# One weight split listed earlier in VectorE's fixed order at the start of the down projection

## The chip, the cores and the metric

The kernel runs on one core of one Trainium2 chip. The metric is the device time of one execution in microseconds (us): a median of 1360.73 us over three runs, from 1359.66 to 1361.09. An execution was also profiled; its rows are quoted below. Line numbers such as L129 are lines of the kernel before; behind the change, the lines from 899 on stand three lower.

## The reference, cut to what matters

One layer of a hybrid encoder block: a short convolution beside an attention head group, an output projection, a gated MLP with a width-3 convolution over positions, a gated embedding, and a last norm. 1024 positions, 1024 channels, 2816 hidden channels of the MLP, all in float32.

```python
    x = x + jnp.concatenate([y_conv, y_mla], axis=-1) @ w_o[i]
    hf = rmsnorm(x, norm_ffn_g[i])
    a = dwconv_centred(hf @ w_up[i], ffn_conv_w[i], ffn_conv_b[i])
    g, u = jnp.split(a, 2, axis=-1)
    x = x + (jax.nn.silu(g) * u) @ w_down[i]
    gate = jax.nn.sigmoid(rmsnorm(x, ple_norm_g[i]) @ w_ple_gate[i])
    x = x + gate * (p[i] @ w_ple_proj[i])
    return rmsnorm(x, final_norm_g)
```

The change is in the line with `w_down`, the down projection, at its very beginning.

## The kernel before, in words

Activations lie transposed: channels on the 128 partitions, 1024 positions along the free axis. A float32 product is made of three products of a shorter type: each operand is split into a high part (a cast, done by ScalarE, ACT) and a low part (the value minus its high part, done by VectorE, DVE), and `gemm` issues high x high, high x low and low x high. With two halves of 512 positions, that is six matmuls per 128x128 block of weights, in this order: weight high with input high (twice), weight high with input low (twice), weight low with input high (twice).

The up projection computes 22 hidden chunks of 128 channels, one unit after the other. Each unit is seven products of sub-blocks (the steps 1 to 7 of a Strassen-like scheme) that go to PSUM banks; DVE adds the banks up (L790), the convolution takes one ACT and two DVE instructions (L261, L262, L263), DVE multiplies the two branches (L810), and SP (the sync engine's DMA queue) writes the chunk to a buffer `gud` in DRAM (L811). The last unit's step 4 comes last on TensorE (PE).

The down projection reads the chunks back in groups of 3, 3, 3, 3, 3, 3 and 4. For a group, `chunk(g)` loads one chunk into a tile `tmp` (L884) and splits it into two tiles `gu` (cast on ACT, L267; subtraction on DVE, L268). `pair(j)` loads the group's weights for two of the eight output tiles into a tile `wraw` (L120, three buffers) and splits them into `whi` (ACT, L128) and `wlo` (DVE, L129), two buffers each. For the first two output tiles the kernel first runs the group's chunks 0 and 1 for both, then chunk 2 for both; the other output tiles run all three chunks one after the other. The finished banks are added by DVE to the residual tiles `x0` to `x7` (L921), which the GpSimd queue (POOL) has loaded back from DRAM (L893).

What sets the order: PE runs in program order through the whole kernel. DVE is in program order too from L892 to the end of the first group (`order0`); each of its instructions keeps the place in which the code lists it, relative to others of that stretch. The compiler's list scheduler decides, by its own time model, how this list is merged with what is still open of the up projection, and it orders ACT, POOL and SP. [...]

The lines around the change: L896 to L898 make the group's chunks, L901 to L906 define `pair`, and L906 and L908 call `pair(0)` and, in the first group, `pair(1)`.

Of the kernel before, what the change touches and what calls it, by code (L numbers as in the profile page):

```python
# [33 lines left out]
def tile_block(ctx, tc, xT, pT, wlat, wun, wdn, wuq, wukv, vecs, cst, out):  # L34
# [25 lines left out]
    def ft(dt=F32, shape=None):  # L60
        return tpool[0].tile(shape or [P, S], dt, name="tmp")
# [12 lines left out]
    def pieces(acc):  # L74
        if isinstance(acc, list):
            return [(acc[i], HALF[i]) for i in range(2)]
        return [(acc, slice(0, S))]
# [37 lines left out]
    def vc(i):  # L115
        return vec[:, i:i + 1]
# [8 lines left out]
    def load_unit(src, n=1024, to=None):  # L125
        raw = load_raw(src, n)
        wh, wl = to or (wp.tile([P, n], FR, name="whi"), wp.tile([P, n], FR, name="wlo"))
        act(out=wh, in_=raw, func=AF.Copy)  # L128
        loeng[0].tensor_tensor(out=wl, in0=raw, in1=f(wh), op=ALU.subtract)  # L129
        return wh, wl  # L130
# [14 lines left out]
    def blocks(acc, w, base, xh, xl, ks, n):  # L145
        for k in ks:
            c = slice((base + k) * P, (base + k) * P + P)
            gemm(acc, w[0][:, c], w[1][:, c], xh[k], xl[k], k == 0, k == n - 1)
# [117 lines left out]
    def split(src, hi, lo, eng=None):  # L266
        nc.scalar.copy(out=hi, in_=src)  # L267
        (eng or nc.gpsimd).tensor_tensor(out=lo, in0=src, in1=f(hi), op=ALU.subtract)  # L268

    def split_gain(x, g, hi, lo):  # L270
        act(out=hi, in_=x, func=AF.Copy, scale=g)
        stt(out=lo, in0=x, scalar=g, in1=f(hi), op0=ALU.mult, op1=ALU.subtract)
# [36 lines left out]
    for c in range(NC_):  # L309
        raw = load_raw(wlat[c], 448)  # L310
        x = ft()
# [473 lines left out]
    def up_unit(c, later=None):  # L785
        raws = [load_raw(wun[U_UP + 2 * c + j]) for j in range(2)]
        mid = lambda n: sp.tile([P, n * 512], FR, name=f"wm{n}", bufs=6 if n == 2 else 4)
        a = stationary(raws[0], raws[1], 512, mid, lambda m: sp.tile([P, S], F32, name=m), later)
        ag, au = tmp.tile([P, S], F32, name="tmp"), tmp.tile([P, S], F32, name="tmp")
        add = lambda o, p, q: tt(out=o, in0=p, in1=q, op=ALU.add)  # L790
        out_, half = [], []

        def read(i, p):
            g1, g2, u1, u2 = ag[:, T1S], ag[:, T2S], au[:, T1S], au[:, T2S]
            if i == 1:
                nc.scalar.copy(out=u1, in_=p)
            elif i == 5:
                add(u2, p, u1)
            elif i == 2:
                nc.scalar.copy(out=g1, in_=p)  # L800
            elif i == 7:
                add(u2, p, u2)
            elif i in (3, 6):
                add(g2, p, g2 if half else u1)
                half.append(i)
            else:
                add(u1, p, u1)
                tpool[0] = tmpb
                t = conv3(au, V_FW + 6 * c + 3, V_FB + 2 * c + 1)
                tt(out=t, in0=out_[0], in1=t, op=ALU.mult)  # L810
                nc.sync.dma_start(out=gud[c], in_=t)  # L811
            if i in (3, 6) and len(half) == 2:
                tpool[0] = tmpb
                t = conv3(ag, V_FW + 6 * c, V_FB + 2 * c)
                act(out=t, in_=t, func=AF.Silu)
                out_.append(t)
        return Unit(a, hf, read)

    pair = [up_unit(0)]
# [14 lines left out]
    def bank():  # L834
        return pb.tile([P, 512], F32, name="bk")
# [39 lines left out]
    def gate_unit():  # L875
        d = len(wg)
        wg.append(load_unit(wun[U_GATE + d], to=(gt(), gt()) if d < 6 else None))
# [4 lines left out]
    def chunk(g):  # L882
        y = ft()
        nc.sync.dma_start(out=y, in_=gud[starts[g] + len(chunks[g])])  # L884
        chunks[g].append((gt(), gt()))
        split(y, *chunks[g][-1], nc.vector)
# [7 lines left out]
    for g, n in enumerate(GROUPS):  # L894
        last = g == len(GROUPS) - 1
        gu = chunks[g]  # L896
        while len(gu) < n:
            chunk(g)  # L898
        gh, gl = [x[0] for x in gu], [x[1] for x in gu]
        ws = []  # L900

        def pair(j):
            if j < 4:
                c = 2 * P * (4 * starts[g] + j * n)
                ws.append(load_unit(wdn[:, c:c + 2 * n * P], 2 * n * P))
        pair(0)  # L906
        if g == 0:
            pair(1)  # L908
        for d in range(NC_):
            if d % 2 == 0:  # L910
                if g and d:
                    pair(d // 2)
                w = ws[d // 2]
            if d == 0:
                p01 = [[bank(), bank()] for _ in range(2)]
                for i in range(2):
                    blocks(p01[i], w, i * n, gh, gl, range(2), n)
            p = p01[d] if d < 2 else [bank(), bank()]
            blocks(p, w, d % 2 * n, gh, gl, range(2 if d < 2 else 0, n), n)
            for q, s in pieces(p):  # L920
                tt(out=x1[d][:, s], in0=q, in1=x1[d][:, s], op=ALU.add)  # L921
            if g == 0 and d % 2:
                pair(d // 2 + 2)
            elif g == 0 and d:
                chunk(1)
            if last:
                hh.append(xp.tile([P, S], FR, name=f"hh{d}"))
                hl.append(xp.tile([P, S], FR, name=f"hl{d}"))
                split_gain(x1[d], vc(V_PLE + d), hh[d], hl[d])
                if d in (1, 3, 5):  # L930
                    gate_unit()
        if g == 0:
            order0.close()
# [214 lines left out]
```

## Time and profile before

| what | value |
|---|---|
| median of three runs | 1360.73 us (1359.66 to 1361.09) |
| the profiled execution, its own time | 1358.89 us |
| its span, first to last instruction | 1357.1 us |
| PE busy | 1322.0 us, 97% of the span |
| DVE busy | 1005.8 us, 74% |
| ACT busy | 597.2 us, 44% |
| POOL busy | 261.1 us, 19% |
| mean granted clock of TensorE | 0.99 |
| up projection ends, down projection begins on PE | 998.69 us after the start of the span |

A row of the waits reads: engine and line that waited, what ended the wait, the total in us, how often, the longest. A row of the timeline reads: start in us, duration in us, engine, line, operation, output <- inputs, how many, and in brackets the idle time before it and what ended that. Neighbouring instructions of one kind are merged into one row; the duration then runs from the first one's start to the last one's end. A matmul of 512 columns is shown with about 0.40 us, but the next one starts some 0.23 us after it, because they overlap in the pipeline. A row of the windows reads: the stretch, its length, busy time of the engine with its number of instructions, then the granted clock of TensorE as a share of full speed, the busy share of the DMA engines, and GB/s.

### The profile page before, as it was taken

To read this page: it belongs to the slowest core of one execution; us is meant where nothing else is said; L and a number is where in the kernel's file an instruction comes from. 1 tells how busy PE (TensorE), PEld (TensorE's weight loads), DVE (VectorE), ACT (ScalarE), POOL (GpSimd) and SP (SyncE) were. 2 spreads that over 40 slices of the span, in tenths; PEclk is the share of its full clock that TensorE was granted. 3 is DMA by queue.
4 is the path that set the end of the run, shared out by engine and by line. 5 is a ranking of instruction groups with operands and counts; after the bars stand their busy time and mean duration, and the time that the engine had idled before them with its cause. 6 is when DMAs were issued, how large, how long until landed. Compare 5 with 4: busy or idle time off the path is not lost.

```text
span 1357.1 us, 16460 instructions
## 1 busy us (share of the span) xinstructions
PE 1322.0 (97%) x6354; PEld 1087.3 (80%) x6354; DVE 1005.8 (74%) x1336; ACT 597.2 (44%) x839; POOL 261.1 (19%) x222
## 2 busy tenths in 40 slices
PE   9999999999999999879999999999989999999997
PEld 7877788888888887658888888888868888888897
DVE  7478923799999956988877888788666555557787
ACT  5323322788888834543343434344432111125433
POOL 0286452455545500000000000000010000000000
PEclk9999999999999999979999999999989999999999
DMA  6201134200000254203222222222274333121123
GB/s 215 78 31 47 47 134 146 78 1 17 1 17 1 81 200 170 93 23 117 78 78 80 91 78 78 78 93 74 69 280 164 94 95 98 57 78 48 54 78 118
DMA packets 38895, 117.38 MB, mean 86 GB/s; under 512 B 4257, under 2 KB 9633, under 8 KB 38817
## 3 DMA queue, kind: packets, MB, share of 16 engines
q1 hardware_dynamic: 35824, 107.30, 22.7%
q10 hardware_dynamic: 1840, 4.83, 0.9%
q0 software_dynamic: 1152, 4.19, 0.8%
q8 instruction: 50, 0.82, 0.2%
q14 instruction: 29, 0.23, 0.0%
HBM read 88.00 MB, written 28.31 MB: 86 GB/s over the span
## 4 chain that ended last, share of the span: by engine, by line
PE 85%; DVE 9%; issue 2%; POOL 2%; ACT 1%; DMA 0%; POOLq 0%; ACTq 0%; SPq 0%
PE bk L139 56%; PE big L139 9%; PE small L139 4%; PE small L534 4%; PE small L547 2%; PE big L504 2%; PE big L508 2%; PE big L506 2%; PE small L546 2%; DVE tmp L163 1%; DVE tmp L262 1%; DVE tmp L263 1%; DVE xt L726 1%; DVE b L726 1%; DVE rbc L164 1%
## 5 line engine op out<-in xcount | busy, mean ns | idle before, releaser
L139 PE MATMUL bk<-b,wm 128*128 128x512 f32 x792 | 192.8, 396 | 1.7 <-DVE b L726 1.4
L139 PE MATMUL bk<-gu,whi 128*128 128x512 f32 x704 | 193.8, 397 | 0.0
L139 PEld LDWEIGHTS bk<-b,wm 128*128 128x128 f32 x792 | 148.5, 188 | 38.7 <-DVE b L726 2.5
L139 PEld LDWEIGHTS bk<-gu,whi 128*128 128x128 f32 x704 | 132.9, 189 | 32.2
L921 DVE TENSOR_TENSOR x<-bk,x 128x512 f32<-128x512 f32 x112 | 72.2, 686 | 96.4 <-PE bk L139 95.7
L139 PE MATMUL bk<-xt,wm 128*128 128x512 f32 x528 | 129.3, 399 | 7.6 <-DVE xt L726 5.4
L128 ACT ACTIVATE whi<-wraw 128x1024 fp32r<-128x1024 f32 (+2 forms) x55 | 51.3, 933 | 192.0 <-PE bk L139 140.3
L139 PEld LDWEIGHTS bk<-xt,wm 128*128 128x128 f32 x528 | 100.8, 192 | 32.6 <-DVE xt L726 7.8
L139 PE MATMUL bk<-gu,wlo 128*128 128x512 f32 x352 | 111.7, 398 | 5.9 <-DVE wlo L129 5.9
L139 PE MATMUL bk<-b,whi 128*128 128x512 f32 x352 | 112.4, 400 | 3.1 <-DVE b L726 3.1
L646 POOL TENSOR_TENSOR wm<-wraw,wm 128x512 fp32r<-128x512 f32 x22 | 28.8, 1309 | 449.0 <-ACT wm L645 449.0
L790 DVE TENSOR_TENSOR tmp<-bk,tmp 128x512 f32<-128x512 f32 x110 | 75.6, 687 | 35.4 <-PE bk L139 35.2
L521 POOL TENSOR_SCALAR tmp<-tmp,sm 128x256 f32<-128x256 f32 x64 | 70.1, 1096 | 101.3 <-DVE sm L514 98.7
L261 ACT ACTIVATE tmp<-tmp,vec 128x1024 f32<-128x1024 f32 x44 | 54.4, 1237 | 71.0 <-DVE tmp L790 71.0
L511 DVE TENSOR_REDUCE mx<-big 128x1 f32<-128x1024 f32 x64 | 78.0, 1218 | 10.3 <-PE big L508 9.8
L139 PEld LDWEIGHTS bk<-gu,wlo 128*128 128x128 f32 x352 | 66.5, 189 | 22.4 <-DVE wlo L129 6.3
L537 DVE TENSOR_TENSOR ptl<-small,pth 128x512 fp32r<-128x512 f32 x128 | 83.1, 679 | 1.2 <-ACT pth L536 0.9
L139 PEld LDWEIGHTS bk<-b,whi 128*128 128x128 f32 x352 | 66.8, 190 | 20.3 <-DVE b L726 4.2
L262 DVE SCALAR_TENSOR_TENSOR tmp<-tmp,vec 128x1023 f32<-128x1023 f32 x48 | 63.9, 1331 | 21.6 <-ACT tmp L261 19.2
L536 ACT CAST pth<-small 128x512 fp32r<-128x512 f32 x128 | 69.0, 591 | 19.8 <-PE small L534 17.4
L513 ACT ACTIVATE tmp<-big,mx 128x1024 f32<-128x1024 f32 x64 | 72.1, 1127 | 5.2 <-DVE sm L514 2.6
L139 PE MATMUL big<-hh,whi 128*128 128x512 f32 x224 | 71.0, 397 | 3.3 <-DVE tmp L414 3.1
(291 smaller groups left out, 2792.5 us busy)
## 6 DMA issues: line engine op xcount, KB each, us to landing
wraw<-in_wun_dram SPq DMA_DIRECT2D x73, 512.0 KB, 3.2
gud<-tmp SPq DMA_DIRECT2D x22, 512.0 KB, 2.6
tmp<-gud SPq DMA_DIRECT2D x22, 512.0 KB, 4.1
wraw<-in_wdn_dram SPq DMA_DIRECT2D x24, 384.0 KB, 3.2
tmp<-in_xT_dram SPq DMA_DIRECT2D x15, 512.0 KB, 4.1
x1d<-tmp SPq DMA_DIRECT2D x8, 512.0 KB, 2.8
xt<-x1d SPq DMA_DIRECT2D x8, 512.0 KB, 6.4
x2d<-xt SPq DMA_DIRECT2D x8, 512.0 KB, 2.7
```

The source lines that it names most:

```text
L128: act(out=wh, in_=raw, func=AF.Copy)
L139: mm(p, w, x[:, s], start=a, stop=z, skip_group_check=more)
L261: act(out=t, in_=src, func=AF.Identity, scale=vc(w + 1), bias=vc(bias))
L262: stt(out=t[:, 1:S], in0=src[:, 0:S - 1], scalar=vc(w), in1=t[:, 1:S], op0=ALU.mult, op1=ALU.add)
L511: nc.vector.tensor_reduce(m, p, AX.X, ALU.max, negate=True)
L513: act(out=e, in_=p, func=AF.Exp, bias=m, accum_out=su)
L521: nc.gpsimd.tensor_scalar(out=e[:, w:S], in0=e[:, w:S], scalar1=su, scalar2=None, op0=ALU.mult)
L534: nc.tensor.transpose(t[:, k, :], e[:, (g * 4 + k) * P:(g * 4 + k) * P + P], ident)
L536: nc.scalar.copy(out=pth[:, ks, qs], in_=t)
L537: tt(out=ptl[:, ks, qs], in0=t, in1=f(pth)[:, ks, qs], op=ALU.subtract)
L790: add = lambda o, p, q: tt(out=o, in0=p, in1=q, op=ALU.add)
L921: tt(out=x1[d][:, s], in0=q, in1=x1[d][:, s], op=ALU.add)
```

## The change

In the first group, `pair(0)` is listed before the three chunks instead of behind them. In every other group it stays where it was, and `pair(1)` of the first group stays behind the chunks.

```diff
     for g, n in enumerate(GROUPS):
         last = g == len(GROUPS) - 1
         gu = chunks[g]
-        while len(gu) < n:
-            chunk(g)
-        gh, gl = [x[0] for x in gu], [x[1] for x in gu]
         ws = []
 
         def pair(j):
             if j < 4:
                 c = 2 * P * (4 * starts[g] + j * n)
                 ws.append(load_unit(wdn[:, c:c + 2 * n * P], 2 * n * P))
-        pair(0)
         if g == 0:
+            pair(0)
+        while len(gu) < n:
+            chunk(g)
+        if g:
+            pair(0)
+        else:
             pair(1)
+        gh, gl = [x[0] for x in gu], [x[1] for x in gu]
```

DVE, in unit 20 of the up projection (L790 adds a bank, L810 ends a unit, L646 makes the low part of a later step's weights). The rows with a plus sign are those of the changed kernel; `wlo_8173` is the low part of the first pair there.

```order
 L790 TENSOR_TENSOR tmp_7884<-bk_7932,tmp_7884 128x512
 L810 TENSOR_TENSOR tmp_7912<-tmp_7852,tmp_7912 128x1024
+L129 TENSOR_TENSOR wlo_8173<-wraw_8170,whi_8172 128x768
 L790 TENSOR_TENSOR tmp_7884<-bk_7918,tmp_7884 128x512
 L646 TENSOR_TENSOR wm2_8009<-s23_7999,wm2_8008 128x1024
```

The first pair's subtraction now stands behind the L810 of the last unit but two (unit 19 of 0 to 21), ahead of the addition of a bank of unit 20 and of a weight split of unit 21 (`wm2_8009`).

DVE, end of the up projection, some fifteen instructions later. Before, the low parts of the chunks 0, 1 and 2 are `gu_8173`, `gu_8179` and `gu_8185`, and the first and second pair's are `wlo_8191` and `wlo_8197`; after, the chunks' are `gu_8179`, `gu_8185` and `gu_8191`.

```order
-L268 TENSOR_TENSOR gu_8173<-tmp_8170,gu_8172 128x1024
+L268 TENSOR_TENSOR gu_8179<-tmp_8176,gu_8178 128x1024
 L262 SCALAR_TENSOR_TENSOR tmp_8118<-tmp_8016,vec_71,tmp_8118 128x1023
 L790 TENSOR_TENSOR tmp_8017<-bk_8051,tmp_8017 128x512
-L268 TENSOR_TENSOR gu_8179<-tmp_8176,gu_8178 128x1024
+L268 TENSOR_TENSOR gu_8185<-tmp_8182,gu_8184 128x1024
 L263 SCALAR_TENSOR_TENSOR tmp_8118<-tmp_8016,vec_71,tmp_8118 128x1023
 L262 SCALAR_TENSOR_TENSOR tmp_8136<-tmp_8017,vec_71,tmp_8136 128x1023
-L268 TENSOR_TENSOR gu_8185<-tmp_8182,gu_8184 128x1024
-L129 TENSOR_TENSOR wlo_8191<-wraw_8188,whi_8190 128x768
+L268 TENSOR_TENSOR gu_8191<-tmp_8188,gu_8190 128x1024
 L129 TENSOR_TENSOR wlo_8197<-wraw_8194,whi_8196 128x768
```

The chunks' subtractions stay where they were, under other numbers; only the row of `wlo_8191` is gone from this place.

SP, around the first load of a chunk (L884). `wraw_8194`, `wraw_8244` and `wraw_8300` are the raw weights of the second, third and fourth pair.

```order
 L811 DMA gud_4864<-tmp_7779 128x1024
 L120 DMA wraw_8194<-in_wdn_dram 128x768
 L120 DMA wraw_8244<-in_wdn_dram 128x768
 L811 DMA gud_4864<-tmp_7912 128x1024
-L884 DMA tmp_8170<-gud_4864 128x1024
+L120 DMA wraw_8300<-in_wdn_dram 128x768
 L884 DMA tmp_8176<-gud_4864 128x1024
+L884 DMA tmp_8182<-gud_4864 128x1024
 L811 DMA gud_4864<-tmp_8045 128x1024
```

The fourth pair's load, which took the first pair's buffer behind all loads of the first two groups' chunks, now stands ahead of them; the loads of the chunks 0 and 1 follow it as they did, under other numbers. On ACT the casts of the first two pairs and of the first group's chunks keep their places, and the fourth pair's cast (`whi_8302`) moves one place up, from behind the cast of the second group's second chunk to ahead of it. PE and POOL keep their order.

## The prediction

> **What bounds the kernel now.** I read the page first: the span, and the chain of work that ended last.
>
> ```profile
> span 1357.1 us, 16460 instructions
> ...
> PE 85%; DVE 9%; issue 2%; POOL 2%; ACT 1%; DMA 0%; POOLq 0%; ACTq 0%; SPq 0%
> ```
>
> PE carries 85% of the chain, so a change elsewhere matters only where PE waits. The second view is the waits of PE (in all, how many, the longest), the third the chain in order of time from there on.
>
> ```profile
> PE bk L139 <- DVE wlo L129: 5.9, 1, 5.9
> ```
>
> ```profile
> 1004.75 0.88 DVE wlo L129
> 1005.63 0.04 issue
> 1005.67 264.70 PE bk L139 x1127
> ```
>
> The longest wait of PE in the whole execution is a single one of 5.9 us on a `wlo` of L129, the instruction that the change moves. It ends at 1005.67. Behind it, PE runs 264.70 us without a wait, then goes on likewise: whatever PE gains at 1005.67, it gains for the end, unless something that now is early enough becomes late. Fourth, PE's timeline around the wait:
>
> ```profile
> 990.34 5.76 PE L139 MATMUL bk<-b,wm 128*128 128x512 f32 x24
> 995.94 2.91 PE L139 MATMUL bk<-xt,wm 128*128 128x512 f32 x12
> 998.69 1.10 PE L139 MATMUL bk<-gu,whi 128*128 128x512 f32 x4
> 1005.67 1.22 PE L139 MATMUL bk<-gu,wlo 128*128 128x512 f32 x2 [5.89 <-DVE wlo L129]
> 1006.69 1.91 PE L139 MATMUL bk<-gu,whi 128*128 128x512 f32 x4
> 1008.40 0.89 PE L139 MATMUL bk<-gu,wlo 128*128 128x512 f32 x2
> 1009.12 1.09 PE L139 MATMUL bk<-gu,whi 128*128 128x512 f32 x4
> ```
>
> 24 matmuls take from 990.34 to 995.94: 0.233 us from one start to the next. The four at 998.69 are high x high and high x low of chunk 0, so the fifth, the first that reads `wlo`, could start at 998.69 + 4 x 0.233 = 999.62. It starts at 1005.67, 6.05 us late (5.89 counted from the modelled end of the fourth). Then eight matmuls (2 + 4 + 2) take until 1009.12, 3.45 us where 8 x 0.233 = 1.87 would do: another 1.58 us. The granted clock tells why:
>
> ```profile
> 1002.00:1003.00 1.00, 0.00 (x0) 0.56 0.98 385
> ...
> 1008.00:1009.00 1.00, 1.00 (x4) 0.53 1.02 414
> ```
>
> The mean clock of 0.56 between 1002 and 1003 means full speed for the first 0.12 us and half behind it, so the clock falls at 1002.1, after 2.3 us of idleness; likewise it returns shortly before 1009. So the wait costs 6.05 + 1.58 = **7.63 us** in all.
>
> **The change, part by part.** First, is `wlo` late only because it is listed late? DVE and ACT at this place:
>
> ```profile
> 996.75 1.22 DVE L268 TENSOR_TENSOR gu<-tmp,gu 128x1024 fp32r<-128x1024 f32 x1
> ...
> 998.08 1.04 ACT L267 CAST gu<-tmp 128x1024 fp32r<-128x1024 f32 x1
> ...
> 1000.01 1.22 DVE L268 TENSOR_TENSOR gu<-tmp,gu 128x1024 fp32r<-128x1024 f32 x1
> ...
> 1001.91 1.05 ACT L267 CAST gu<-tmp 128x1024 fp32r<-128x1024 f32 x1 [0.54 <-DMA tmp<-gud]
> ...
> 1003.53 1.22 DVE L268 TENSOR_TENSOR gu<-tmp,gu 128x1024 fp32r<-128x1024 f32 x1
> 1004.66 1.82 DVE L129 TENSOR_TENSOR wlo<-wraw,whi 128x768 fp32r<-128x768 f32 x2
> ```
>
> and at the place to which the instruction moves:
>
> ```profile
> 969.27 1.21 DVE L810 TENSOR_TENSOR tmp<-tmp 128x1024 f32<-128x1024 f32 x1
> ...
> 970.84 0.85 ACT L128 ACTIVATE whi<-wraw 128x768 fp32r<-128x768 f32 x1 [5.15 <-PE bk L139]
> ...
> 973.88 0.69 DVE L790 TENSOR_TENSOR tmp<-bk,tmp 128x512 f32<-128x512 f32 x1 [3.40 <-PE bk L139]
> 974.73 1.23 DVE L646 TENSOR_TENSOR wm<-s,wm 128x1024 fp32r<-128x1024 f32 x1 [0.16 <-ACT wm L645]
> ```
>
> The high part of the first pair is cast at 970.84, ready at 971.69; its low part waits 33 us more in DVE's list behind the three chunks. In the new list it follows the L810 that ends at 970.48. It starts when the cast ends, 971.7, takes about 0.95 (half of 1.82, with the overlap) and ends at 972.7. DVE sat idle there until 973.88, so **moving it in costs nothing**: 1.2 us of cover are left. If that cover were gone, each further us would be handed to the bank addition at 973.88 and the split at 974.73. At the old place 0.95 us leaves DVE's queue, and the second pair's `wlo` ends at 1005.6.
>
> Second, **what is late next.** The fifth and sixth matmul now start at 999.62, the two of chunk 1's high part at 1000.09 (it is cast by 998.08 + 1.04 = 999.12). The next two read chunk 1's low part, which DVE ends at 1000.01 + 1.22 = 1001.23; PE could start them at 1000.56. With the 0.04 of the chain's "issue" row, PE waits until 1001.27: 0.71 us. This instruction's inputs do not depend on the change: chunk 1's cast stands on ACT, and the additions ahead of it on DVE, as before. From 1001.27 PE needs 4 matmuls for the rest of that block, 12 for the second output tile and 2 for chunk 2's high part, 18 x 0.233 = 4.2, so chunk 2's low part is wanted at 1005.5; it is there at 1003.53 + 1.22 = 1004.75. Slack 0.7 us. The second pair is wanted at 1007.9 and is there at 1005.6.
>
> How a wait as short as 0.71 us acts on the clock, rows from the beginning of the up projection show (its timeline, then the windows, where the third number from the right is the granted clock):
>
> ```profile
> 560.20 3.53 PE L139 MATMUL bk<-b,wm 128*128 128x512 f32 x14 [0.96 <-DVE b L726]
> 563.57 0.63 PE L139 MATMUL bk<-b,whi 128*128 128x512 f32 x2
> ...
> 568.75 0.80 PE L139 MATMUL bk<-b,whi 128*128 128x512 f32 x1 [2.08 <-DVE b L726]
> ```
>
> ```profile
> 560.20:564.00 3.80, 3.80 (x16) 3.12 (x17) 3.80 (x6) 1.48 (x2) 0.00 (x0) 1.00 0.01 2
> ...
> 568.70:572.00 3.30, 3.25 (x8) 2.56 (x9) 3.08 (x5) 1.14 (x2) 0.00 (x0) 0.50 0.00 0
> ```
>
> After 0.96 us of waiting the clock is still 1.00; 14 matmuls take 563.57 - 560.20 = 3.37 instead of 3.27, 0.10 for getting under way. After 2.08 it is 0.50. I take the first, as 0.71 is nearest to it, and keep half speed as the other bound.
>
> **The sum:** 7.63 - 0.71 - 0.10 = **6.8 us gained** at PE. [...]
>
> Third, **the moved transfer.** On SP the fourth pair's load now stands ahead of chunk 0's. It waits for the first pair's buffer, free at 972.7:
>
> ```profile
> 970.51 0.33 SPq L811 DMA_DIRECT2D gud<-tmp  x1
> 981.43 6.26 SPq L884 DMA_DIRECT2D tmp<-gud  x2
> ...
> 997.99 7.10 SPq L884 DMA_DIRECT2D tmp<-gud  x4
> ```
>
> SP is idle from 970.84 to 981.43, so the load goes out at 972.7 with 8.7 us to spare, and chunk 0's load keeps its time. It also leaves its old place behind the four loads of 997.99, where the DMA engines are full (the shares of 0.98 and 1.02 above). That is no gain for PE, which waits there for no transfer.
>
> Fourth, **can the rest follow 6.8 us earlier?** PE then begins the third output tile at about 1007.9. A tile is three blocks of six matmuls, so the fifth, which needs the third pair, begins at 1007.9 + 36 x 0.233 = 1016.3.
>
> ```profile
> 997.82 3.89 POOL L893 DMA_DIRECT2D x<-x2d  x7 [33.25 <-PE bk L139]
> ...
> 1008.29 1.05 ACT L267 CAST gu<-tmp 128x1024 fp32r<-128x1024 f32 x1 [4.38 <-DMA tmp<-gud]
> 1014.45 0.85 ACT L128 ACTIVATE whi<-wraw 128x768 fp32r<-128x768 f32 x1 [5.11 <-PE bk L139]
> ```
>
> ```profile
> DMA to landing us min/median/max: 5.1/9.7/14.8
> ```
>
> The third pair's cast, which PE releases at 1014.45 now, would be released at 1007.9; it then stands behind the cast that waits for a transfer until 1008.29 and ends at 1009.3, so it is done at 1010.2. Its `wlo` on DVE stands behind the additions to x0 and x1; if x1 landed as late as the slowest of these loads (the last row, for the eight of L893, the first of them sent at 997.82), at some 998.4 + 14.8 = 1013.2, then 1.3 for its addition and 0.95 for the split would make it 1015.5, still ahead of 1016.3. The fourth pair's cast, now one place earlier on ACT, waits for PE as before. Nothing else there is paced by anything but PE. Cost: none.
>
> The profiled execution took 1358.89 us, 1.84 below the median of the runs; it would take 1352.1. Moved to the median, 1360.73 - 6.8 = **1353.9 us**.
>
> **The rivals.** (a) *The short wait still drops the clock.* Then eight matmuls at half speed come back, 1.58 us, and the time is 1355.5. For it: the clock fell after 2.1 us, and what decides could be a share of idleness rather than its length. Against: the 1.00 after 0.96 us.
>
> (b) *Another input was the last one.* The profile puts the wait down to `wlo` alone; if chunk 2's low part (1004.75) or all of DVE's list held PE too, only 1005.63 - 1004.75 = 0.9 us would go, and 1359.8 would remain. For it: the two end close together. Against: PE's program reads chunk 2 only after 24 matmuls of the chunks 0 and 1.
>
> (c) *Slower: chunk 2's load loses the race with the x loads.* It is sent at 997.99, amid the eight loads of POOL, and lands about 1001.9 now, with 0.7 us of slack on PE's side that the old wait had hidden. Loads of this kind took 3.1 to 11.6 us to land, by the row of their tile:
>
> ```profile
> DMA to landing us min/median/max: 3.1/7.0/11.6
> ```
>
> At 11.6 it lands at 1009.6, the cast and the split end at 1009.6 + 1.05 + 1.22 = 1011.9, and PE waits from 1005.5 on for 6.4 us and again pays about 1.6 for the clock: 1353.9 + 8.0 = 1361.9, slower than before. The point from which it decides is a landing of 5.2 us (5.2 + 1.05 + 1.22 behind 997.99 is 1005.5); slower than before it becomes at about 10.4, and by more than 0.2% from 13 on. Against: what is sent ahead of it is sent at the same times, and the one load that moved leaves.
>
> (d) *DVE is held at the moved instruction.* It now waits for a cast with 1.2 us of cover, and PE would notice only when the split at 974.73 slips by more than some 6 us: it is wanted by step 6 of the last unit, 12 matmuls behind the start of this row, at 982.1.
>
> ```profile
> 979.28 5.63 PE L139 MATMUL bk<-xt,wm 128*128 128x512 f32 x24
> ```
>
> So the cast would have to end 7 us later than now, and each further us is a us of time: with 14 us, 1360.9, as before. [...]
>
> That the change does not do what it says is ruled out by the order: one `wlo` moves.
>
> **How the numbers follow.** Forecast 0.80, (a) 0.08, (b) 0.06, (c) 0.04, (d) 0.02. The forecast's own spread is that of the runs, some 0.7 to each side for both medians, some 1.0 together; with no short wait at all (0.8 less) that is 1352.1, so the range begins at 1352.0. At its upper end it takes in (a) with that spread, 1356.4. Some 0.12 are left above, little below. A measurement of this kernel can tell about 0.2%, 2.7 us, from no change. Faster by more: the forecast, (a) and (d) where it costs little, 0.90. Within: (b) and a quarter of (c), 0.07. Slower: the rest of (c), 0.03.
>
> **What would show it.** In the changed kernel's profile: the `wlo` of 128x768 alone near 971.7 on DVE and one L120 of SP near 972.7; the bank addition still at 973.9; PE's longest wait in the down projection about 0.7 us on a `gu` of L268 near 1001.2; a granted clock of 1.00 throughout 999 to 1010; the first addition to x0 (L924 there) near 1008, as it stands behind an L810; the chain of PE behind it unbroken, and the span at about 1350.3. Wrong it would be if PE showed a wait on `gu` of several us, a new one on `wlo` at 1016, or half the clock near 1002.

## The result, and the profile after

The changed kernel takes 1353.12 us (median of six runs, 1352.51 to 1354.2) against 1360.68 us for the kernel before (six runs on the same chip, 1359.3 to 1361.9). The medians differ by 7.6 us. The ratio is 0.9946, with a 95% interval from 0.9933 to 0.9959, which is 5.6 to 9.1 us less. The forecast was 1353.9 us, with a range from 1352.0 to 1356.4.

The page of the changed kernel and its waits of PE (in all, how many, the longest):

```profile
span 1350.6 us, 16462 instructions
...
PE 85%; DVE 9%; issue 2%; POOL 2%; ACT 1%; DMA 0%; POOLq 0%; SPq 0%; ACTq 0%
```

```profile
PE bk L139 <- DVE gu L268: 0.6, 1, 0.6
```

The single wait of 5.9 us on `wlo` is gone from the list; in the down projection one of 0.6 us is left, on a chunk's low part. PE's timeline, to be laid beside the one of before:

```profile
996.28 2.91 PE L139 MATMUL bk<-xt,wm 128*128 128x512 f32 x12
999.02 1.10 PE L139 MATMUL bk<-gu,whi 128*128 128x512 f32 x4
999.96 0.63 PE L139 MATMUL bk<-gu,wlo 128*128 128x512 f32 x2
1000.43 0.63 PE L139 MATMUL bk<-gu,whi 128*128 128x512 f32 x2
1001.62 0.72 PE L139 MATMUL bk<-gu,whi 128*128 128x512 f32 x2 [0.56 <-DVE gu L268]
1002.18 0.63 PE L139 MATMUL bk<-gu,wlo 128*128 128x512 f32 x2
1002.64 1.10 PE L139 MATMUL bk<-gu,whi 128*128 128x512 f32 x4
```

The first four matmuls, then the two with `wlo`, follow without a gap. The eight matmuls that were done at 1009.12 - 998.69 = 10.43 us behind the first one of the down projection are now done at 1002.64 - 999.02 = 3.62: **6.81 us** earlier. The granted clock at the place of the rest of the wait:

```profile
1001.00:1002.00 1.00, 0.44 (x3) 1.00 1.01 414
```

It stays at 1.00. The moved instruction, its cast and what stands behind it:

```profile
969.60 1.21 DVE L810 TENSOR_TENSOR tmp<-tmp 128x1024 f32<-128x1024 f32 x1
972.06 0.96 DVE L129 TENSOR_TENSOR wlo<-wraw,whi 128x768 fp32r<-128x768 f32 x1 [1.24 <-ACT whi L128]
974.21 0.69 DVE L790 TENSOR_TENSOR tmp<-bk,tmp 128x512 f32<-128x512 f32 x1 [1.20 <-PE bk L139]
```

and the fourth pair's load on SP:

```profile
970.84 0.33 SPq L811 DMA_DIRECT2D gud<-tmp  x1
973.04 0.33 SPq L120 DMA_DIRECT2D wraw<-in_wdn_dram  x1
981.83 6.21 SPq L884 DMA_DIRECT2D tmp<-gud  x2
```

DVE waits 1.24 us for the cast and 1.20 more for PE behind it: it would have been idle there either way. This execution began the down projection 0.33 us later than the one of before, and all these rows lie 0.33 to 0.40 later for that reason alone.

That late start has to be taken out of every comparison below. Executions of these kernels differ by up to 2.2 us in when the down projection begins. All of it is there already at about 614 us, far ahead of the change: a matmul that starts there starts 384.72 us before the down projection in each of the twelve executions. So I measure the stretch from the first matmul of the down projection to the first matmul of the later norm (L178), which the chain of waits gives, first of before, then of the changed kernel:

```profile
1270.38 0.23 PE bk L178
```

```profile
1263.90 0.23 PE bk L178
```

| kernel | begins at | L178 at | stretch, us |
|---|---|---|---|
| before | 998.69 | 1270.38 | 271.69 |
| before, two more executions | 999.09, 998.98 | 1271.19, 1271.03 | 272.10, 272.05 |
| changed | 999.02 | 1263.90 | 264.88 |
| first pair behind chunk 0 | 999.92 | 1265.33 | 265.41 |
| first pair behind chunks 0 and 1, two executions | 1000.87, 998.89 | 1269.10, 1267.12 | 268.23, 268.23 |
| both pairs first | 999.24 | 1264.12 | 264.88 |
| changed, chunks in turn for the two tiles | 999.28 | 1263.49 | 264.21 |
| changed, tile 0 whole before tile 1, two executions | 1000.58, 1000.18 | 1267.58, 1267.19 | 267.00, 267.01 |
| before, with 24 filling matmuls | 999.38 | 1269.59 | 270.21 |

In the two experiments that were profiled twice, the stretch repeats to 0.01 us, which makes differences of half a microsecond readable that the runs' times cannot tell.

### The profile page after: what moved, and what is told of

Its sections match the earlier page's. It is cut to its first block, busy times and chain, and to the rows that moved or that the text cites. A ratio compares the mean times of both kernels' runs of the same rounds, so it can differ in the third digit from the quotient of the medians.

```text
span 1350.6 us, 16462 instructions
## 1 busy us (share of the span) xinstructions
PE 1321.4 (98%) x6354; PEld 1086.6 (80%) x6354; DVE 1005.5 (74%) x1336; ACT 596.8 (44%) x839; POOL 260.8 (19%) x222
## 4 chain that ended last, share of the span: by engine, by line
PE 85%; DVE 9%; issue 2%; POOL 2%; ACT 1%; DMA 0%; POOLq 0%; SPq 0%; ACTq 0%
PE bk L139 56%; PE big L139 9%; PE small L139 4%; PE small L534 4%; PE small L547 2%; PE big L504 2%; PE big L508 2%; PE big L506 2%; PE small L546 2%; DVE tmp L163 1%; DVE xt L726 1%; DVE tmp L263 1%; DVE tmp L262 1%; DVE b L726 1%; DVE rbc L164 1%
## 5 line engine op out<-in xcount | busy, mean ns | idle before, releaser
L646 POOL TENSOR_TENSOR wm<-wraw,wm 128x512 fp32r<-128x512 f32 x22 | 28.9, 1312 | 449.3 <-ACT wm L645 449.3
L790 DVE TENSOR_TENSOR tmp<-bk,tmp 128x512 f32<-128x512 f32 x110 | 75.5, 686 | 33.5 <-PE bk L139 33.5
```

## The experiments

The theory to be tested: the place of the first pair's split in DVE's list is all that mattered. The cost of the old place had two terms, the wait and the half clock behind it; behind that PE paces everything, so the gain reaches the end whole. The rivals: the transfer that moved on SP is what gained; the half clock is not caused by the wait; something other than the two low parts holds PE.

**The first pair behind chunk 0.**

```diff
         if g == 0:
+            while len(gu) < 1:
+                chunk(g)
             pair(0)
```

> The first pair is listed behind chunk 0 and ahead of chunks 1 and 2. In the order, its low part then stands on DVE behind chunk 0's subtraction, and the fourth pair's load goes back among the loads behind chunk 2's. My theory (the place in DVE's list is all): the low part ends near 999.3, before PE wants it at 999.96, so PE has no wait on it; but it pushes chunk 1's subtraction back by about 0.6 us, so the wait on chunk 1's low part grows from 0.72 to some 1.3 us, the clock stays at 1.00, and the time is 0.6 above the changed kernel's 1353.1: 1353.7. Rival (the transfer that moved on SP is what gained): with the load back in its crowded place, the time returns to 1360.7. Rival (the clock falls after any wait above 1 us): 1.6 more, 1355.3.

Measured: 1353.64 us, ratio 0.9952 (0.9939 to 0.9966); the stretch is 0.53 us above the changed kernel's.

```profile
997.98 1.22 DVE L268 TENSOR_TENSOR gu<-tmp,gu 128x1024 fp32r<-128x1024 f32 x1
999.12 0.95 DVE L129 TENSOR_TENSOR wlo<-wraw,whi 128x768 fp32r<-128x768 f32 x1
...
1001.78 1.21 DVE L268 TENSOR_TENSOR gu<-tmp,gu 128x1024 fp32r<-128x1024 f32 x1
```

```profile
1003.05 0.73 PE L139 MATMUL bk<-gu,whi 128*128 128x512 f32 x2 [1.10 <-DVE gu L268]
```

`wlo` is done at 1000.07, before PE wants it at 1000.86, and the whole loss is chunk 1's low part, pushed back: 1.10 us of idleness in place of 0.56. And the transfer is back where it was crowded, at 1000.09, between the loads of the chunks (the share of the DMA engines was 0.89 and 1.07 from 1001 to 1003):

```profile
999.22 0.32 SPq L884 DMA_DIRECT2D tmp<-gud  x1
1000.09 0.33 SPq L120 DMA_DIRECT2D wraw<-in_wdn_dram  x1
1003.02 3.84 SPq L884 DMA_DIRECT2D tmp<-gud  x3
```

Nearly the whole gain without the early transfer: that rival falls.

**The first pair behind chunks 0 and 1.** The same edit with a 2.

> The first pair is listed behind chunks 0 and 1 and ahead of chunk 2. My theory: its low part runs on DVE right behind chunk 1's subtraction, from about 1001.5 to 1002.4; PE, which wants it at 999.96, waits about 2.35 us from the modelled end of its last matmul. The wait on chunk 1 is gone (it is split by then). Against the changed kernel's wait of 0.72 that is 1.7 to 1.8 more at full clock: 1354.9. The idle time is at the point where the clock fell in the kernel before (2.1 to 2.3 us): if it falls, eight matmuls at half speed add up to 1.6, and the time is up to 1356.5. Rival (only the whole wait of 6 us counts, since it is a transfer or chunk 2 that PE needs): 1359 to 1360.7.

Measured: 1357.43 us, ratio 0.9975 (0.9965 to 0.9985); the stretch is 3.35 us above the changed kernel's and 3.46 below that of before.

```profile
1000.87 1.10 PE L139 MATMUL bk<-gu,whi 128*128 128x512 f32 x4
1004.33 0.91 PE L139 MATMUL bk<-gu,wlo 128*128 128x512 f32 x2 [2.36 <-DVE wlo L129]
```

The wait is the 2.36 us expected. At full clock that makes 1.7 more than in the changed kernel; the other 1.6 is the clock, which did fall: it was 0.50 in each us from 1005 to 1008. One chunk later in DVE's list costs 0.5 us, two cost 3.35, three (the kernel before) 6.8. The median lies 0.9 us above the upper end expected, 1356.5. In the profiled execution, 1.9 us were lost by 54 us: a matmul that starts at 51.2 to 51.7 us in most executions started at 53.45. Whether that holds for the other runs is not known; the second execution of this kernel, without that loss, took 1355.65.

**The clock without the wait.** Matmuls that nothing reads fill PE's wait in the kernel before (`tiny` is a list of actions that `gemm` takes up, two behind each matmul).

```diff
                 p01 = [[bank(), bank()] for _ in range(2)]
+                if g == 0:
+                    fill = bank()
+                    tiny.extend([lambda: None] * 7)
+                    tiny.append(lambda: [mm(fill, w[0][:, 0:P], gh[0][:, 0:512], start=True, stop=True) for _ in range(24)])
```

> The kernel before, with 24 matmuls whose result nothing reads put on PE where it waits for the first pair's low part (behind the fourth matmul of the down projection, into a free bank). Everything else stands as before; the result is the same. My theory (the cost of the wait has two terms, 6.05 us of waiting and 1.58 of half clock behind it): the low part still ends at 1005.6, PE is busy for 24 x 0.233 = 5.6 us of the time and waits about 0.4, the clock stays at 1.00, and only the second term goes: the eight matmuls behind take 1.9 to 2.0 instead of 3.45 us, 1.5 us gained, 1359.2. Rival (the half clock is not caused by idleness but by the place, for instance by the load of the DMA engines): 1360.7, the eight matmuls still take 3.45.

Measured: 1358.75 us, ratio 0.9993 (0.9984 to 1.0002), which by itself tells nothing from no change; the stretch is 1.48 us shorter than that of before.

```profile
1000.32 5.76 PE L919 MATMUL bk<-gu,whi 128*128 128x512 f32 x24
1006.37 0.72 PE L139 MATMUL bk<-gu,wlo 128*128 128x512 f32 x2 [0.29 <-DVE wlo L129]
1006.93 1.10 PE L139 MATMUL bk<-gu,whi 128*128 128x512 f32 x4
1007.86 0.63 PE L139 MATMUL bk<-gu,wlo 128*128 128x512 f32 x2
1008.33 1.10 PE L139 MATMUL bk<-gu,whi 128*128 128x512 f32 x4
```

The first matmul with `wlo` starts 1006.37 - 999.38 = 6.99 us behind the first one, as before (6.98), so the wait is the same; but the eight behind it take 1008.33 - 1006.37 = 1.96 us instead of 3.45, at a granted clock of 1.00 in each us from 1006 to 1009, where the kernel before had 0.50, 0.50 and 0.53. The second term is the clock, and here it hung on PE's idleness: the place is the same, and the DMA engines were as full (shares of 0.98 and 1.00 in the two stretches that the prediction shows with 0.98 and 1.02). After the stretch this execution lost another 0.5 us against before, so its span (1356.8) shows only part of the gain; why is open.

**The rest of the wait.** In the changed kernel, chunk 0 for both tiles, then chunk 1 for both:

```diff
-                for i in range(2):
-                    blocks(p01[i], w, i * n, gh, gl, range(2), n)
+                for k in range(2):
+                    for i in range(2):
+                        blocks(p01[i], w, i * n, gh, gl, [k], n)
```

> The changed kernel, with the first two chunks run for both output tiles in turn (chunk 0 for tile 0, chunk 0 for tile 1, then chunk 1 for both) in place of tile by tile. My theory: the rest of the wait is chunk 1's low part alone, which is then wanted 1.4 us later, at 1002.3, and is there at 1001.6; the 0.72 us and the 0.1 behind it go, and nothing takes their place but chunk 2's low part, wanted at 1005.1 and ready at 1005.1: at most 0.1. Time 1352.4, a span of about 1349.9. Rival (PE cannot begin earlier than something else allows, such as the banks or the x loads): the wait comes back elsewhere and the time stays at 1353.1.

Measured: 1352.12 us, ratio 0.9942 (0.9929 to 0.9954); the stretch is 0.67 us shorter than the changed kernel's.

```profile
1003.49 1.09 PE L139 MATMUL bk<-gu,whi 128*128 128x512 f32 x4
1004.42 0.63 PE L139 MATMUL bk<-gu,wlo 128*128 128x512 f32 x2
1004.89 1.24 PE L139 MATMUL bk<-gu,whi 128*128 128x512 f32 x4
1005.96 0.63 PE L139 MATMUL bk<-gu,wlo 128*128 128x512 f32 x2
```

No wait is left but a trace of the one on chunk 2's low part: the four matmuls at 1004.89 take 1.24 us instead of 1.09. This is the best version of the study, though by the times alone it cannot be told from the changed kernel.

**Chunk 2 wanted earlier.** In the changed kernel, all three chunks for tile 0, then for tile 1, in the first group:

```diff
-                for i in range(2):
-                    blocks(p01[i], w, i * n, gh, gl, range(2), n)
+                if g:
+                    for i in range(2):
+                        blocks(p01[i], w, i * n, gh, gl, range(2), n)
...
-            blocks(p, w, d % 2 * n, gh, gl, range(2 if d < 2 else 0, n), n)
+            blocks(p, w, d % 2 * n, gh, gl, range(2 if g and d < 2 else 0, n), n)
```

> The changed kernel, with all three chunks run for output tile 0 before tile 1 in the first group, so that chunk 2 is wanted 12 matmuls earlier. My theory: chunk 2's high part is wanted at 1002.6 and cast at 1003.3 (0.7 us of wait), its low part is wanted 0.5 later and ready at 1005.1 (1.3 us more): 2.0 us at full clock, 1355.1. With the 0.56 us ahead of it that makes some 2.6 us of idleness in pieces within 4.2 us: if the share of idleness decides the clock, and not one long wait, it falls to half near 1005, and up to 1.6 us are added: 1356.7. Rival (chunk 2's load has slack that the profile does not show, since its cast is only listed late): no more than 0.5 us, 1353.6.

Measured: 1357.23 us, ratio 0.998 (0.9971 to 0.9989); the stretch is 2.12 us above the changed kernel's, at a granted clock of 1.00 in each us from 999 to 1011.

```profile
1003.17 0.74 PE L139 MATMUL bk<-gu,whi 128*128 128x512 f32 x2 [0.56 <-DVE gu L268]
1003.74 0.62 PE L139 MATMUL bk<-gu,wlo 128*128 128x512 f32 x2
1004.85 0.74 PE L139 MATMUL bk<-gu,whi 128*128 128x512 f32 x2 [0.49 <-ACT gu L267]
1006.70 0.73 PE L139 MATMUL bk<-gu,whi 128*128 128x512 f32 x2 [1.10 <-DVE gu L268]
```

The two new waits are chunk 2's high part (ended by ACT) and its low part (ended by DVE), as the forecast had them behind 24 matmuls with 0.7 us of slack. Twelve matmuls are 12 x 0.233 = 2.8 us; less the 0.7 of slack that leaves 2.1, which is what the stretch lost. The interleaving that the kernel already had is what hides them. The median lies above both times expected, 1355.1 at full clock and 1356.7 with a fall; by the time alone one would have said that the clock fell, and the profile denies it with its 1.00. It says where the rest went in the profiled executions: this execution began the down projection at 1000.58 and ended 0.8 us later behind L178 than the changed kernel's; the second began at 1000.18 and ended 0.5 later. By 54 us the first was already late by some 1.7 us. Neither part has been explained.

**Both pairs first.**

```diff
         if g == 0:
             pair(0)
+            pair(1)
         while len(gu) < n:
             chunk(g)
         if g:
             pair(0)
-        else:
-            pair(1)
```

> The changed kernel with the second pair listed ahead of the chunks too. Its low part then stands on DVE behind the last unit but one's L810, waits there for its cast until about 991.5 and ends at 992.5, ahead of a bank addition that PE releases at 993.7. My theory: PE does not wait for it in the changed kernel, DVE has cover there too, so nothing moves on PE: its wait stays 0.6 to 0.7 us on chunk 1's low part, and the time is 1353.1. Rival (DVE is held at the instruction and the bank additions behind it slip): a loss of 1 us per us of slip on chunk 1's subtraction, 1354 or more. Rival (DVE's end at 1008.4 sets the additions to x, and so the banks): 1 us gained, 1352.2.

Measured: 1354.28 us, ratio 0.9958 (0.9944 to 0.9972); the stretch is 264.88 us, the changed kernel's to the hundredth. The median is 1.2 us above the changed kernel's and in the range of the first rival, but the intervals of the two ratios overlap, and the stretch shows no loss.

```profile
988.91 1.22 DVE L810 TENSOR_TENSOR tmp<-tmp 128x1024 f32<-128x1024 f32 x1
991.74 0.96 DVE L129 TENSOR_TENSOR wlo<-wraw,whi 128x768 fp32r<-128x768 f32 x1 [1.62 <-ACT whi L128]
993.90 0.69 DVE L790 TENSOR_TENSOR tmp<-bk,tmp 128x512 f32<-128x512 f32 x1 [1.20 <-PE bk L139]
```

The second pair's split waits at the head of DVE's list for its cast, and 1.20 us of cover are left behind it, as for the first. A wait that ended within an idle stretch of its engine cost nothing here; and a DVE that is 0.95 us earlier at 1005 brought nothing.

**The half clock in other executions.** Two more executions of the kernel before, and one each of two of the experiments.

> The kernel before, looked at once more, for the term of 1.58 us. [...] Theory L (a fixed length of idleness, then a fixed length of work): the clock falls 2.1 to 2.3 us behind the last matmul, returns 3.3 us behind the first, and the loss is 1.6 us again. [...]

> [...]

> All three chunks for tile 0 before tile 1, looked at once more. [...] Theory L: never a fall, since no wait is over 1.1 us.

> The first pair behind chunks 0 and 1, looked at once more. In its first profile a wait of 2.36 us let the clock fall 0.4 us after PE had begun again. [...] Theory L: a fall every time, 268.2.

In its two further executions the kernel before waited 5.89 us for `wlo` again. Two stretches of its second execution, at the fall of the clock and at its return:

```profile
1003.00:1004.00 1.00, 0.00 (x0) 0.72 1.05 422
1010.00:1011.00 1.00, 1.00 (x5) 0.87 1.07 434
```

The stretches between 1004 and 1010 have 0.50. With full speed for one part of the us and half for the other, the clock fell at 1002.12 in the first execution and at 1003.44 in the second. The last matmul ahead of the wait ended at 999.79 in the first execution and 1000.19 in the second; the clock fell 2.3 and 3.25 us behind it (in the third, 3.1). And it returned at 1008.94, 3.27 us behind the matmul that ended the wait, and at 1010.26, 4.18 behind it. The half clock thus cost 1.6 us in the first execution and 2.1 in the second, and the stretch is 0.41 us longer. In the third it is 0.36 longer. Theory L falls: neither the 2.1 to 2.3 us nor the 3.3 us was met again.

The two repeated experiments came out as theory L has them too, and so say nothing more against it. The second execution with the pair behind two chunks waited 2.36 us, the clock fell again (0.69 in the stretch from 1002 to 1003, 0.50 in the two behind it), and its stretch is 268.23 us, the 268.2 expected. The second with tile 0 first had waits of 0.56, 0.59 and 1.02 us and stayed at 1.00. How much idleness makes the clock fall, and what sets the moment, no run here shows.

## Why the prediction was right

*The wait and its two terms.* Forecast: 6.05 us of waiting and 1.58 of half clock. The filling matmuls took the second away alone and moved the stretch by 1.48.

*Moving it in costs nothing.* The split ran at 972.06, with 1.20 us of cover behind it; the bank addition kept its distance from the step that releases it. Right, and right for the second pair also.

*What is late next.* Forecast: chunk 1's low part, 0.71 us late and 0.10 for getting under way. In the starts, PE could have gone on at 1000.43 + 2 x 0.233 = 1000.90 and did so at 1001.62: 0.72. That this is all is shown by the order in turn, which removed it and gained 0.67.

*Chunk 2's slack.* The forecast put 0.7 us between its low part and its use. With the order in turn, where PE arrives 0.8 us earlier, it is just used up, and with tile 0 first it is exceeded by 2.1.

*The sum.* 6.8 us forecast; 6.81 measured between the two profiles. That it agrees to a hundredth is in part luck, since the sum was sized from the same execution of before with which it is compared here. The median moved by 7.6, with 6.8 inside its interval. The other two executions of before lost 0.4 us more to the clock, so that against them the sum would be 7.2. The term of the half clock was sized from one execution at 1.58, and that execution lay at the low end: the three give 1.6, 2.1 and 2.0.

*The moved transfer.* Forecast: no gain and no loss. It went out at 973.04, 8.8 us ahead of the next load; the version without it lost only what chunk 1 explains.

*Can the rest follow?* The additions and the third pair's cast of the changed kernel:

```profile
1008.40 2.48 DVE L924 TENSOR_TENSOR x<-bk,x 128x512 f32<-128x512 f32 x4
1008.78 1.05 ACT L267 CAST gu<-tmp 128x1024 fp32r<-128x1024 f32 x1 [4.49 <-DMA tmp<-gud]
1009.73 0.84 ACT L128 ACTIVATE whi<-wraw 128x768 fp32r<-128x768 f32 x1
1010.79 0.95 DVE L129 TENSOR_TENSOR wlo<-wraw,whi 128x768 fp32r<-128x768 f32 x1
```

The four additions follow each other without a wait for a transfer, so x0 and x1 were there in time, and the third pair is ready at 1011.7, with nearly 5 us to spare until 1016.6. Right.

*The rivals.* (a), the clock falls after the short wait, did not happen: it stayed at 1.00 through the wait of 0.56 us. Whether a share of idleness decides, which spoke for it, was not shown. (b) falls with the positions, which take the cost back in steps. (c) did not happen; the load lands in the same 3.9 us. (d) did not happen either.

*What was wrong* are two readings on the way. One is the term of the half clock, read from one execution as if it held for all. There the clock fell 2.3 us into the wait and returned 3.27 us behind its end; in the other two executions it fell 3.25 and 3.1 us into the same wait and returned 4.18 and 4.05 us behind its end. The other is the choice of the row with the 0.96 us wait as a sign that a short wait leaves the clock alone. In the second execution of before, the clock fell during that very wait, and the 14 matmuls behind it took 564.78 - 560.03 = 4.75 us instead of 3.37:

```profile
560.03 4.92 PE L139 MATMUL bk<-b,wm 128*128 128x512 f32 x14 [0.96 <-DVE b L726]
564.78 0.63 PE L139 MATMUL bk<-b,whi 128*128 128x512 f32 x2
```

```profile
559.00:559.50 0.50, 0.07 (x1) 1.00 0.06 16
559.50:560.00 0.50, 0.00 (x0) 0.71 0.06 25
560.00:560.50 0.50, 0.47 (x1) 0.50 0.04 16
```

The conclusion held all the same: the clock was 1.00 through the short wait at 1001. Why it fell at the one wait and not at the other was not shown.

## What to carry to other kernels

Where an engine's order is written by hand, what the consumer wants first belongs first in the list, and what is ready long before belongs into an idle stretch of the engine: one subtraction of 0.95 us, listed behind those of three chunks, cost 7 us. A wait of the matrix engine is to be priced with the half clock that may follow it, which added a quarter to a third here, and from more than one execution, since behind the same wait it cost 1.6, 2.1 and 2.0 us in three. And when the longest wait is taken away, the next input in line decides what is gained; its time can be read from the old profile if it does not depend on the change.

## What the runs showed that was not expected

In one execution the granted clock fell when PE had already begun again: with the pair behind two chunks, PE resumed at 1004.33 and the clock fell 0.39 us later, at 1004.72.

```profile
1004.00:1005.00 1.00, 0.67 (x2) 0.86 0.91 352
```

A wait of 2.36 us thus cost 1.6 us more than its length in that kernel, while with tile 0 whole before tile 1 three waits of 0.56, 0.49 and 1.10 us, 2.15 together, with work between them, left the clock at 1.00.
